# A two-layer decoder trunk on one core: the ten split-weight buffers each at another place within 128 bytes

## The chip, the core and the metric

The kernel runs on one core of a Trainium2 chip. The metric is the device time of one execution in microseconds; the time of a kernel is the median of its runs. Five engines work side by side: TensorE (PE in the profile; PEld are its weight loads), VectorE (DVE), ScalarE (ACT), GpSimd (POOL) and SyncE (SP), which issues the transfers from the chip's main memory. Each takes its own instructions in program order.

## The reference

A decoder of two layers over 256 tokens of width 1024, in float32. Each layer is a token mixer with two kinds of attention in parallel, and a SwiGLU:

```python
proj = x @ w_in      # q, k, v of 8 stick-breaking heads, q, k, v of 8 MoBA heads, two gates
branch_sb = merge_heads(stick_breaking(q_sb, k_sb, v_sb)) @ w_branch_sb
branch_mb = merge_heads(moba(rope(q_mb), rope(k_mb), v_mb)) @ w_branch_moba
mix = (sigmoid(g_sb) * branch_sb + sigmoid(g_mb) * branch_mb) @ w_out
x = layer_norm(ALPHA * x + mix)
x = layer_norm(ALPHA * x + (silu(x @ w_gate) * (x @ w_up)) @ w_down)
```

## The kernel before, in words

The matrix products are done in pieces of 128 rows. To keep float32 accuracy with TensorE's faster 32-bit type, every operand is split into a rounded part (`hi`) and the rest (`lo`), and every product is three matmuls into one bank, written out in `mm3` (L281): hi x hi, hi x lo, lo x hi. All matmuls but the transposes are issued on L275.

The weights of a layer are cut into 122 *granules* of 128 partitions x 1024 float32, 4096 bytes in each partition. `WeightStream.line` takes one granule after another: a transfer into one of four `raw` buffers (L119), the rounded copy `whi` by ScalarE (L145), the rest `wlo` = `raw` - `whi` by VectorE (L149). There are ten buffers for `whi` and ten for `wlo`, and granule g uses buffer g modulo 10 (`NSPLIT`). A granule may be split once the one ten places ahead of it has had its last matmul (`allow`).

A granule is used in one of two ways. A matmul has a *stationary* operand of 128 x 128, which a weight load brings into the array while the matmul before it still runs, and a *moving* operand that streams past it.

- `feat_major` (L327) and the branch projections (L671 on): the weights are stationary, eight slices of 128 columns (512 bytes) per granule, and 256 tokens move. A granule is 24 matmuls of 256 columns. This holds for the q and k of stick-breaking (`pqk`), the gates (`pg`), the branch projections (`pb`) and most of the SwiGLU input (`pf`).
- `tok_major` (L305) and `token_out` (L336): the activations are stationary, and up to 512 columns of the weights move. This holds for `pv`, `pq`, `pk`, `pu`, `pvq`, `pft`, the output projection `pw` and the down projection `pd` and `pe`.

In these names l0 or l1 ahead is the layer. `xT_hi` and `xT_lo` are the transposed tokens.

The order of all instructions is fixed when the program is built, by `Weave`: it walks along the matmuls with an estimate of every engine's clock and puts in the side work (attention, norms, rotary, splits) where its operands should be there. The addresses play no part in this order.

All tiles lie in pools of on-chip memory, at addresses set when the program is built. `xT_hi`, `xT_lo` are in the pool `const`, at a multiple of 128 bytes. The weight buffers follow in `wpool`: four `raw`, ten `whi`, ten `wlo`, each 4096 bytes, all of them at byte 64 of 128. The pools `acts` (attention outputs, gates, SwiGLU outputs, fifteen tiles of 4096 bytes) and `work` come behind it, their large tiles too at byte 64 of 128.

Of the kernel before, what the change touches and what calls it, by code (L numbers as in the profile page):

```python
# [8 lines left out]
F32R = mybir.dt.float32r  # L9
# [5 lines left out]
P = 128  # L15
# [14 lines left out]
GCOLS = 1024  # L30
# [4 lines left out]
class Weave:  # L35
    """Program order: the main line of projections, with side lines (attention, norms,
    rotary, weight splits) woven in. Every engine takes its instructions in program order,
    so each is emitted about when its operands are there, by an estimate of the time at
    which each engine gets through what it has been given. A side line yields the time
    at which it goes on; on the tensor engine's clock."""  # L40

# [40 lines left out]
    def start(self, gen):  # L82
        """A side line whose first stage comes now."""
        side = self.add(gen)
        if not self.busy:
            self._step(side)
        return side
# [9 lines left out]
class WeightStream:  # L97
    """Weight granules [128, 1024]: loaded in float32, then split exactly into
    two float32r parts (hi = rounded, lo = the rest) for the tensor engine."""

# [13 lines left out]
    def load(self, upto):  # L114
        while self.loaded < min(upto, self.total):
# [7 lines left out]
            self.loaded += 1  # L123

    def line(self):
        """The side line: a granule at a time, as far as the buffers allow."""
        nc, weave = self.nc, self.weave
        while self.split < self.total:
            g = self.split
            ahead = g - self.current  # L130
            if g > self.limit:
                yield weave.t + 0.1
                continue
            if ahead >= LEAD and max(weave.dve_t, weave.act_t) > weave.t + BACKLOG:
                yield weave.t + 0.2
                continue
            self.load(g + NRAW)
            if ahead > 0:
                yield self.there[g]
            hi, lo = (self.pool.tile([P, GCOLS], F32R, tag=n, name=f"{n}{g}", bufs=NSPLIT)  # L140
                      for n in ("whi", "wlo"))
            t = self.raw.pop(g)
            n = GCOLS // len(self._pieces(g))
            for sl in self._pieces(g):
                e = weave.act(self.there[g], n, nc.scalar.copy, hi[:, sl], t[:, sl])  # L145
            if g - self.current > 0:
                yield e
            for sl in self._pieces(g):
                e = weave.dve(e, n, nc.vector.tensor_sub, lo[:, sl], t[:, sl], hi[:, sl].bitcast(F32))  # L149
            self.parts[g], self.ready[g] = (hi, lo), e  # L150
            self.split += 1
            self.load(g + 1 + NRAW)

    def allow(self, g):
        """Granule g's buffers are free from here on."""
        self.limit = max(self.limit, min(g, self.total - 1))
# [9 lines left out]
NRAW = 4  # L166
NSPLIT = 10
HOLD = 8
N_WARM = 7
# [10 lines left out]
def hybrid_trunk_kernel(ctx: ExitStack, tc: tile.TileContext, w, xT_in, x_in, ln_in,  # L180
# [6 lines left out]
    work = ctx.enter_context(tc.tile_pool(name="work", bufs=3))  # L187
# [24 lines left out]

# [1 line left out]
    xT_raw = [unit(f"xT_raw{t}", [P, KC, P]) for t in range(2)]  # L214
# [12 lines left out]
    nc.scalar.activation(warm, zero, AF.Sigmoid)  # L227
    # The tensor engine's clock rises after some microseconds of work: give it zeros meanwhile.
    idle = unit("idle", [P, 512], F32R)
# [42 lines left out]

# [1 line left out]
    def mm(o, a, b, start, stop):  # L274
# [30 lines left out]
    def tok_major(o, g, t, first, last, k0):  # L305
        """o[tokens of t, 512] += x @ granule g ([2 kc, 512])."""
        hi, lo = ws.take(g)
        hi = hi.rearrange("p (k c) -> p k c", k=2)
        lo = lo.rearrange("p (k c) -> p k c", k=2)
        for k in range(2):  # L310
            ts = slice(t * P, (t + 1) * P)
            mm3(o, xT_hi[:, k0 + k, ts], xT_lo[:, k0 + k, ts], hi[:, k, :], lo[:, k, :],
                first and k == 0, last and k == 1)

    def both_tokens(name, g0, put):
        """All tokens of x @ granules g0..g0+3; put(tokens, bank) takes each half."""
        acc = [bankM(f"{name}{t}", [P, WIDTH]) for t in range(2)]
        order = ((0, 0), (1, 0), (0, 1), (1, 1), (0, 2), (0, 3)) if g0 == 0 else \
            ((0, 0), (0, 1), (0, 2), (1, 0), (1, 1), (0, 3))
        for t, k in order + ((1, 2), (1, 3)):  # L320
            tok_major(acc[t], g0 + k, t, k == 0, k == 3, 2 * k)
            if t == 1:
                ws.allow(g0 + k + NSPLIT)
            if k == 3:
                put(t, acc[t])

    def feat_major(o, g):  # L327
        """o[128 columns, 256 tokens] = (x @ granule g)^T, g [8 kc, 128 columns]."""
        hi, lo = ws.take(g)
        hi = hi.rearrange("p (k c) -> p k c", k=KC)  # L330
        lo = lo.rearrange("p (k c) -> p k c", k=KC)
        for k in range(KC):
            mm3(o, hi[:, k, :], lo[:, k, :], xT_hi[:, k, :], xT_lo[:, k, :], k == 0, k == KC - 1)
        ws.allow(g + NSPLIT)

    def token_out(o, g, t, s_hi, s_lo, first, last):  # L336
        """o[tokens of t, 1024] += s^T @ granule g ([1 kc, 1024]); o: (first column, bank) ..."""
        hi, lo = ws.take(g)
        ts = slice(t * P, (t + 1) * P)
        for c0, ps in o:  # L340
            cs = slice(c0, c0 + ps.shape[-1])
            mm3(ps, s_hi[:, ts], s_lo[:, ts], hi[:, cs], lo[:, cs], first, last)

    ROWS = [(slice(h * DH, (h + 1) * DH), slice((1 - h) * DH, (2 - h) * DH)) for h in range(2)]

    # Per head, q is stacked as [hi; lo] over the 128 rows and each part of k is there twice,
    # so that q k^T = q_stack (k_hi twice) + q_stack (k_lo twice).
    def stack_q(qs, src, n, c, e):
        """qs[head] [128, ...] from src [2 heads x 64, ...]; the second head is [lo; hi]."""
        for h, (a, b) in enumerate(ROWS):  # L350
            e = act(e, n, nc.scalar.activation, qs[h][a], src[a], AF.Copy, scale=c)
        yield e
        for h, (a, b) in enumerate(ROWS):
            dve(e, n, nc.vector.scalar_tensor_tensor, qs[h][b], src[a], c, qs[h][a].bitcast(F32),
                op0=OP.mult, op1=OP.subtract)
# [15 lines left out]
    def rope_line(name, ps, t, put):  # L371
        """Token-major q or k (8 heads x 64) -> rotary -> transposed, handed to put."""
        tmp = work.tile([P, 8, DH], F32, tag="T", name=f"{name}_tok{t}")
# [22 lines left out]
    def scores(s, q, kh, kl, m):  # L396
        """Scores of both heads of a pair: columns 0:128 = (q0, k0), 128:384 = (q1, k0 k1),
        with the causal mask m added to the diagonal blocks."""
        for h in range(2):
# [12 lines left out]
    def weighted(name, p, wt, v, oT, e):  # L412
        """oT[:, p] = (wt @ v)^T for both heads of pair p."""
        yield e + MARGIN
# [93 lines left out]
    def scale_shift(e, x, cols, sub, op, scale, g, b, e_scale):  # L508
        """x <- ((x op sub) g) scale + b; yields each piece of columns as it is done."""
        for c in cols:  # L510
# [7 lines left out]
    def norm_line(name, t, junk, gb):  # L518
        """x_t <- LN(alpha x_t + ps) g + b, and its transpose into xT (split)."""
        x = xs[t]  # L520
# [26 lines left out]
    def last_norm(name, t, banks, gb, down):  # L547
        """The output's tokens: LN(alpha x_t + sum) g + b, blocks of columns in turn."""
        x = xs[t]
# [24 lines left out]

# [1 line left out]
    norms = []  # L576
    for l in range(DEPTH):
        G = l * NG_LAYER
        L = f"l{l}"

        # v of stick-breaking and q of MoBA: tokens 0..127 first
        v_sb = pair_tiles(L + "vsb", [P, 2, WIDTH])
# [28 lines left out]

        # Each pair of stick-breaking heads starts with its q and k; k and v of MoBA and the
        # first gates come between, MoBA's heads after the last sigmoid of stick-breaking, and
        # the gates' sigmoids after the last exponential of MoBA.
        o_sb = pair_tiles(L + "osb", [P, NPAIR, S])
# [47 lines left out]

        # branch projections and the gated merge, feature-major
        gb = load_gb(l, 0)
# [20 lines left out]

        # output projection: tokens 0..127 first
        norms = []
# [7 lines left out]

        # SwiGLU, first chunks token-major (tokens 0..127 first)
        h_t = [pair_tiles(f"{L}h{i}", [P, 4, S]) for i in range((NFC + 3) // 4)]
# [47 lines left out]

        # down projection: the last granules' tokens 0..127 first
        gb = load_gb(l, 1)
# [5 lines left out]
        g = G + 100  # L754
# [102 lines left out]
```

## Time and profile before

| | |
|---|---|
| median of 3 runs | 753.91 us |
| lowest and highest run | 753.79 and 755.08 us |
| span of the profiled execution, first to last instruction | 747.6 us |
| bytes moved by transfers | 136.31 MB, mean 182 GB/s |
| mean granted TensorE clock | 0.999 |

The profile gives the span of the profiled execution; the time of the runs has 6.3 us more than that span, before its first and behind its last instruction. Busy time of an engine is the time in which at least one of its instructions ran. A matmul's record covers its way through the array, so records overlap, and the distance between the starts of two matmuls is shorter than the length of one. The chain that ended last lists, in order of time, the stretches of work that set the end, each with its start, its length and its count of instructions.

### The profile page before, as it was taken

What the parts mean: (1) busy time and instruction counts of PE and PEld (TensorE: products, weight loads), DVE (VectorE), ACT (ScalarE), POOL (GpSimd) and SP (SyncE); (2) the same over time, 40 slices, a digit from 0 to 9 for tenths busy, and PEclk for the clock granted to TensorE, in tenths of its full rate; (3) what the DMA queues carried; (4) which work ended last, traced back from release to release, by engine and by line L of the source; (5) the groups of instructions that cost most, each with busy time, mean ns of one, the idle gap of its engine ahead of it and who ended that gap; (6) DMA issues with size and microseconds to landing.
All of it is one profiled execution on the core that took longest, in us unless ns stands there. A gap on an engine that the chain in (4) does not pass through costs nothing.

```text
span 747.6 us, 12689 instructions
## 1 busy us (share of the span) xinstructions
PE 735.1 (98%) x5049; PEld 675.5 (90%) x5049; DVE 529.9 (71%) x772; ACT 421.8 (56%) x655; POOL 13.4 (2%) x20
## 2 busy tenths in 40 slices
PE   8999999999999999999999999999999999999996
PEld 5888999998799999988888889999987999999885
DVE  6897878696886666644488878886768866665416
ACT  6788867744565445433267877777435654554300
POOL 0000000000000000000000000000010000000001
PEclk9999999999999999999999999999999999999999
DMA  8864724554586565676168445345635865657501
GB/s 292 284 217 151 221 93 153 176 199 167 178 265 227 181 194 182 198 241 194 60 196 258 146 162 177 108 145 198 210 113 183 277 201 194 196 185 246 166 1 56
DMA packets 39082, 136.31 MB, mean 182 GB/s; under 512 B 4464, under 2 KB 6000, under 8 KB 39024
## 3 DMA queue, kind: packets, MB, share of 16 engines
q1 hardware_dynamic: 39024, 135.51, 55.6%
q8 instruction: 39, 0.64, 0.3%
q14 instruction: 19, 0.16, 0.1%
HBM read 134.45 MB, written 1.05 MB: 181 GB/s over the span
## 4 chain that ended last, share of the span: by engine, by line
PE 84%; DVE 6%; ACT 3%; DMA 3%; issue 2%; POOL 1%; SPq 0%; POOLq 0%; DVEq 0%; ACTq 0%
PE l0pf L275 14%; PE l1pf L275 13%; PE l0pd L275 8%; PE l1pg L275 6%; PE l0pg L275 6%; PE l1pe L275 4%; PE l1pd L275 4%; PE l1pb L275 3%; PE l0pb L275 3%; PE l1pvq L275 3%; DMA raw<-in_w_dram 3%; PE l1pw L275 2%; PE l0pw L275 2%; PE l1pqk L275 2%; DVE wlo L53 2%
## 5 line engine op out<-in xcount | busy, mean ns | idle before, releaser
L53 DVE TENSOR_TENSOR wlo<-raw,whi 128x1024 fp32r<-128x1024 f32 (+1 forms) x245 | 296.8, 1219 | 93.0 <-ACT whi L48 89.5
L48 ACT CAST whi<-raw 128x1024 fp32r<-128x1024 f32 (+1 forms) x245 | 254.1, 1046 | 86.7 <-PE l0pd L275 22.6
L275 PE MATMUL l0pf<-xT_hi,whi 128*128 128x256 f32 x288 | 81.0, 281 | 0.0
L275 PE MATMUL l0pf<-xT_lo,whi 128*128 128x256 f32 x288 | 80.9, 281 | 0.0
L275 PE MATMUL l0pf<-xT_hi,wlo 128*128 128x256 f32 x288 | 80.9, 281 | 0.0
L275 PE MATMUL l1pf<-xT_hi,whi 128*128 128x256 f32 x288 | 79.6, 276 | 0.0
L275 PE MATMUL l1pf<-xT_lo,whi 128*128 128x256 f32 x288 | 79.5, 276 | 0.0
L275 PE MATMUL l1pf<-xT_hi,wlo 128*128 128x256 f32 x288 | 79.5, 276 | 0.0
L275 PEld LDWEIGHTS l0pf<-xT_hi,wlo 128*128 128x128 f32 x288 | 55.3, 192 | 0.0
L275 PEld LDWEIGHTS l0pf<-xT_lo,whi 128*128 128x128 f32 x288 | 54.1, 188 | 0.0
L275 PEld LDWEIGHTS l1pf<-xT_lo,whi 128*128 128x128 f32 x288 | 54.1, 188 | 0.0
L275 PEld LDWEIGHTS l0pf<-xT_hi,whi 128*128 128x128 f32 x288 | 54.1, 188 | 0.0
L275 PEld LDWEIGHTS l1pf<-xT_hi,whi 128*128 128x128 f32 x288 | 54.1, 188 | 0.0
L275 PEld LDWEIGHTS l1pf<-xT_hi,wlo 128*128 128x128 f32 x288 | 54.1, 188 | 0.0
L275 PE MATMUL l0pg<-xT_hi,whi 128*128 128x256 f32 x128 | 35.9, 281 | 0.0
L275 PE MATMUL l1pg<-xT_hi,whi 128*128 128x256 f32 x128 | 35.9, 281 | 0.0
L275 PE MATMUL l0pg<-xT_lo,whi 128*128 128x256 f32 x128 | 35.5, 277 | 0.0
L275 PE MATMUL l1pg<-xT_lo,whi 128*128 128x256 f32 x128 | 35.5, 277 | 0.0
L275 PE MATMUL l1pg<-xT_hi,wlo 128*128 128x256 f32 x128 | 35.4, 277 | 0.0
L275 PE MATMUL l0pg<-xT_hi,wlo 128*128 128x256 f32 x128 | 35.4, 277 | 0.0
L275 PE MATMUL l0pd<-whi,l0h_hi 128*128 128x512 f32 x88 | 34.4, 391 | 0.0
L275 PE MATMUL l0pd<-whi,l0h_lo 128*128 128x512 f32 x88 | 34.3, 389 | 0.0
(379 smaller groups left out, 1821.1 us busy)
## 6 DMA issues: line engine op xcount, KB each, us to landing
raw<-in_w_dram SPq DMA_DIRECT2D x243, 512.0 KB, 4.1
ln<-in_ln_dram SPq DMA_DIRECT2D x8, 512.0 KB, 7.3
xT_raw<-in_xT_dram SPq DMA_DIRECT2D x8, 128.0 KB, 5.0
x<-in_x_dram SPq DMA_DIRECT2D x2, 512.0 KB, 6.4
out_dram<-x SPq DMA_DIRECT2D x3, 256.0 KB, 2.1
raw<-in_w_dram SPq DMA_DIRECT2D x2, 256.0 KB, 3.7
out_dram<-x SPq DMA_DIRECT2D x2, 128.0 KB, 2.0
mask<-in_mask_dram SPq DMA_DIRECT2D x1, 128.0 KB, 3.2
```

What stands on the lines that cost most here:

```text
L48: f(*args, **kw)
L53: f(*args, **kw)
L275: nc.tensor.matmul(o, a, b, start=start, stop=stop)
```

## The change

Each of the twenty buffers gets a tile of its own, 8 float32 longer than a granule, and the granule's data starts at 0 to 6 float32 within it:

```diff
+    def _part(self, n, g):
+
+        i = g % NSPLIT
+        t = self.pool.tile([P, GCOLS + 8], F32R, tag=f"{n}{i}", name=f"{n}{g}", bufs=1)
+        at = PLACES[i]
+        return t[:, at:at + GCOLS]
+
     def line(self):
...
-            hi, lo = (self.pool.tile([P, GCOLS], F32R, tag=n, name=f"{n}{g}", bufs=NSPLIT)
-                      for n in ("whi", "wlo"))
+            hi, lo = (self._part(n, g) for n in ("whi", "wlo"))
...
 NSPLIT = 10
+PLACES = (0, 0, 4, 4, 0, 2, 4, 6, 1, 5)
```

The rest of the diff blanks docstrings and comments and moves the line numbers by seven. On every engine the instructions, their order and their waits are as before; only addresses differ. A tile is now 4128 bytes, and the tiles lie in the order `whi` 0, `wlo` 0, `whi` 1, `wlo` 1 and so on. The built programs have these starts, in bytes modulo 128:

| buffer | 0 | 1 | 2 | 3 | 4 | 5 | 6 | 7 | 8 | 9 |
|---|---|---|---|---|---|---|---|---|---|---|
| `whi`, before | 64 | 64 | 64 | 64 | 64 | 64 | 64 | 64 | 64 | 64 |
| `wlo`, before | 64 | 64 | 64 | 64 | 64 | 64 | 64 | 64 | 64 | 64 |
| `whi`, after | 64 | 0 | 80 | 16 | 64 | 8 | 80 | 24 | 68 | 20 |
| `wlo`, after | 96 | 32 | 112 | 48 | 96 | 40 | 112 | 56 | 100 | 52 |

`xT`, `raw` and all tiles of `const` stay where they were. `acts`, `work` and `small` lie 640 bytes further on, which is a multiple of 128, so their places within 128 bytes are as before.

## The prediction

> **What bounds the kernel.** I read the page first, then the chain that ended last, then the groups of weight loads and of the two splitting engines.
>
> ```profile
> span 747.6 us, 12689 instructions
> PE 735.1 (98%) x5049; PEld 675.5 (90%) x5049; DVE 529.9 (71%) x772; ACT 421.8 (56%) x655; POOL 13.4 (2%) x20
> ...
> PEclk9999999999999999999999999999999999999999
> ...
> PE 84%; DVE 6%; ACT 3%; DMA 3%; issue 2%; POOL 1%; SPq 0%; POOLq 0%; DVEq 0%; ACTq 0%
> ```
>
> TensorE is busy for 98% of the span, its clock is granted in full, and 84% of the chain that ended last is its own time. So the time is, in the main, the number of matmuls times the distance from one start to the next. The busy figures can't give that distance, since matmuls overlap; the chain can, because it lists unbroken runs with their length and count (start, length, what, count):
>
> ```profile
> 77.56 5.44 PE l0pg L275 x48
> ...
> 83.92 5.65 PE l0pqk L275 x48
> ...
> 90.59 3.75 PE l0pg L275 x33
> ...
> 143.10 23.02 PE l0pb L275 x192
> 166.12 17.04 PE l0pw L275 x75
> ...
> 215.20 99.64 PE l0pf L275 x846
> 314.84 55.08 PE l0pd L275 x243
> ...
> 375.61 6.88 PE l1pvq L275 x30
> ...
> 511.20 23.02 PE l1pb L275 x192
> ...
> 583.38 95.90 PE l1pf L275 x846
> ```
>
> Divide length by count. The SwiGLU projection of layer 0 (`l0pf`) takes 99.64 / 846 = 117.8 ns per matmul, that of layer 1 (`l1pf`) 95.90 / 846 = 113.4 ns: the same code, the same shapes, the same 846. The gates `l0pg` go at 113.3 ns, `l0pqk` six microseconds later at 117.7, and the branch projections `l0pb` and `l1pb` at 119.9, each for 23 us on end. All of these have 256 moving columns. So one shape has three speeds, each of which holds for tens of microseconds. With 512 columns `l0pd` takes 226.7 ns, `l0pw` 227.2 and `l1pvq` 229.3. The weight loads show the same split (count, then busy us and mean ns of one):
>
> ```profile
> L275 PEld LDWEIGHTS l0pf<-xT_hi,wlo 128*128 128x128 f32 x288 | 55.3, 192 | 0.0
> L275 PEld LDWEIGHTS l1pf<-xT_hi,wlo 128*128 128x128 f32 x288 | 54.1, 188 | 0.0
> L275 PEld LDWEIGHTS l0pf<-xT_lo,whi 128*128 128x128 f32 x288 | 54.1, 188 | 0.0
> ...
> L275 PEld LDWEIGHTS l0pb<-l0omb_hi,whi 128*128 128x128 f32 x32 | 6.1, 192 | 0.0
> ```
>
> At the fast pitch every load takes 188 ns; in `l0pf` one of three (the low part) takes 192; in `l0pb` all do. I read this as the two streams that TensorE takes from on-chip memory, the load of the next stationary tile and the moving operand of the running matmul, getting into each other's way at some relative positions. In the projections the load comes from a weight buffer at byte 64 of 128 and the moving operand from `xT` at byte 0; in `l0pb` both are at 64. That the chip does this is a reading of these rows, not shown by them: 113.4 and 117.8 occur with the same addresses, so the position alone doesn't decide it.
>
> A rule speaks against this reading. The Trainium skill, "TensorE: Matmul & The Clock Gate", section "Step-by-step: what each phase is for", says that TensorE has two independent read ports and that loading the next tile's weights takes no bandwidth from the running matmul. By it places could not matter and the sum would be zero; the three pitches at a full clock and the loads of 188 and 192 ns are hard to square with it.
>
> **The change part by part.** No instruction is added, removed or moved, on any engine or queue, and the waits are the same: `whi` and `wlo` turned through ten buffers before, and turn through ten now. What changes is where they lie. Before, all twenty start at byte 64 of 128. After, a tile is 32 bytes longer, so each next one starts 32 bytes further on, and `PLACES` adds 0 to 24 bytes. `whi` of slots 0 to 9 starts at byte 64, 0, 80, 16, 64, 8, 80, 24, 68 and 20, `wlo` 32 bytes further. The other large tiles that TensorE reads keep their place of 128.
>
> *The splitting engines.* ScalarE writes `whi`, VectorE reads it and writes `wlo`:
>
> ```profile
> L53 DVE TENSOR_TENSOR wlo<-raw,whi 128x1024 fp32r<-128x1024 f32 (+1 forms) x245 | 296.8, 1219 | 93.0 <-ACT whi L48 89.5
> L48 ACT CAST whi<-raw 128x1024 fp32r<-128x1024 f32 (+1 forms) x245 | 254.1, 1046 | 86.7 <-PE l0pd L275 22.6 <-PE l1pe L275 20.0 <-PE l0pf L275 14.9
> ...
> L53 DVE TENSOR_TENSOR l0sb_beta<-l0sb_beta,l0sb_inc 128x766 f32<-128x766 f32 x4 | 3.8, 957 | 0.4
> ...
> L53 DVE TENSOR_TENSOR l0sb_pl<-l0sb_pT,l0sb_ph 128x768 fp32r<-128x768 f32 x4 | 3.8, 952 | 0.1
> ...
> PE l0pv L275 <- DVE wlo L53: 1.6, 4, 0.8
> ```
>
> `l0sb_beta` reads `inc` from its second float on, four bytes off, and its 766 elements take 957 ns against 952 for 768 of `l0sb_pl`, which starts on the line. So a shifted VectorE read costs at most 5 ns; for 245 that is 1.2 us, in front of which VectorE stood idle for 93.0. A shifted write is shown nowhere; I take zero, the nearest row. At the upper end, ten per cent on ScalarE's 1046 ns is 26 us, within its 86.7 of idle time. The cover is thin only at the start, where TensorE waits for `wlo` four times, 1.6 us in all; there ten per cent on both is below 1 us. I keep 0 to +1.
>
> *Weights as the stationary operand, 256 columns.* By the code these are 864 `pf`, 384 `pg`, 192 `pqk` and 192 `pb` in each layer, 3264 in all. Now granule after granule has another distance between load and moving operand, for `whi` and `wlo` apart, so no speed is handed on for 36 granules as in `pf`. Which place gives which speed no row shows. With a third of the matmuls at each of the three speeds the mean is (113.4 + 117.8 + 119.9) / 3 = 117.0 ns. Against today: `l0pf` 864 x -0.8 = -0.7 us; `l1pf` 864 x 3.6 = +3.1; `pg`, at 113.6 (3.75 / 33), 768 x 3.4 = +2.6; `pqk`, half at each of 113.3 and 117.7, 384 x 1.5 = +0.6; `pb` 384 x -2.9 = -1.1. Sum +4.5. With half at the fast speed and a quarter at each other the mean is 116.1, and the same five terms are -1.5, +2.3, +1.9, +0.2 and -1.5, together +1.4. I take the middle, **+3 us**. The ends: all at the fast speed is -3.8 for `l0pf`, -2.5 for `pb`, -0.8 for `pqk` and -0.2 for `pg`, so -7.3; all at 119.9 is +1.8, +5.6, +4.8 and +1.7, so +13.9.
>
> *Weights as the moving operand, 512 columns.* 576 matmuls have `xT` as stationary operand (`pv`, `pq`, `pk`, `pu`, `pvq`, `pft`), 654 another tile (`pw`, `pd`, the wide `pe`). The first go at about 229.3 ns, the others at about 226.7. If both kinds come to lie between, they cancel: -576 x 1.3 + 654 x 1.3 = +0.1; I take zero. All at 226.7 is -1.5, all at 229.3 is +1.7. The narrow `pe` matmuls, 132, are worth at most 132 x 6.5 = 0.9 and are left at zero.
>
> Sum: +3 us on the profiled span of 747.6. The median of the runs, 753.9, lies 6.3 above the span, and nothing outside the span is touched: 753.9 + 3 = about **757.0**.
>
> **The rivals.**
>
> *The spread breaks the slow lock (faster).* If most distances are harmless, `l0pf` and `pb` come down to 113.4 and the projections to 226.7: -7.3 - 1.5 = -8.8, so 745, and half of it 749.5. For it: in the chain the gates return to 113 ns after nearly every break, so the fast state seems the natural one. Against it: in `l1pf` and the gates there is nothing left to gain.
>
> *A start off the line costs extra (slower).* Seven of ten slots start off a multiple of 32 bytes. If such a start makes each load one step longer, the step is at most what the slowest pitch has over the fastest, 119.9 - 113.4 = 6.5 ns. On 0.7 of the 2880 `pf`, `pg` and `pqk` that is +13.1, less 2.7 that `l0pf` pays today: +10.4, or 764. If the 512-column matmuls pay too, 0.7 x 1230 x 6.5 = +5.6 more: 770. It turns the result slower from a price of about 2 ns on (0.7 x 2880 x 2 = 4.0, which the 2.7 no longer covers). For it: pitch and loads move in steps of several ns, as a memory with wide lines would give. Against it: no row has such a start on TensorE. The Trainium skill, "SBUF — State Buffer", section "Specifications (TRN2)", gives lines of 16 bytes and a penalty for each cross to a new one; by it a 512-byte load off the line touches 33 lines, not 32, in four of the ten slots. No run here shows that price.
>
> *The places do nothing.* The speed is set by how a run is entered, not by places. Then `l0pf` and `l1pf` fall either way again: -3.8 to +3.8 around 753.9.
>
> **How the numbers follow.** The mixture, my forecast, has 0.45, with 754 to 760 as its own range; the broken lock 0.20; the extra step 0.20; nothing 0.15. About 0.2% (1.5 us) is what a measurement of this kernel can tell from no change. Slower by more: 0.27 of the mixture, 0.20 of the extra step, 0.05 of nothing, together 0.52. Same: 0.12 and 0.06, 0.18. Faster: 0.06, 0.20 and 0.04, 0.30. The range runs from 746, almost the whole gain of the broken lock, to 768, between the two prices of the extra step; some 0.1 lies beyond each end at most.
>
> **What would show it.** In the chain of the changed kernel `l0pf` and `l1pf` should come closer to each other, with runs of about 98.5 us for 846, and no longer keep one pitch: within ten granules the pitch should change with the slot. `pb` should be under 23.0 us for 192. ScalarE's 1046 ns and VectorE's 1219 should stand. If all granules of slots 2, 3 and 5 to 9 are slow and 0, 1 and 4 are not, it is the extra step. If `l0pf` or `l1pf` keeps one pitch throughout, places do nothing. The prediction is wrong if the 512-column runs move by more than 2 ns, or if waits on `wlo` appear.

## The result, and the profile after

| | before | after |
|---|---|---|
| median of the runs | 753.88 us (753.79 to 755.08, 4 runs) | 762.15 us (761.74 to 763.08, 4 runs) |
| span of the profiled execution | 747.6 us | 759.3 us |
| time of the profiled execution | not among the runs | 761.76 us |

The change makes the kernel slower by about 1%: the ratio is 1.0106, with an interval of [1.0091, 1.0121]. The forecast was 757.0 with a range of 746 to 768.

The page of the changed kernel: its span, busy times, granted clock, and the shares of the chain that ended last.

```profile
span 759.3 us, 12689 instructions
...
PE 748.2 (99%) x5049; PEld 684.9 (90%) x5049; DVE 530.9 (70%) x772; ACT 421.6 (56%) x655; POOL 13.4 (2%) x20
...
PEclk9999999999999999999999999999999999999998
...
PE 87%; DVE 4%; ACT 4%; issue 2%; DMA 1%; SPq 1%; POOL 1%; POOLq 0%; DVEq 0%; ACTq 0%
...
L53 DVE TENSOR_TENSOR wlo<-raw,whi 128x1024 fp32r<-128x1024 f32 (+1 forms) x245 | 296.8, 1219 | 95.5 <-ACT whi L48 92.1
L48 ACT CAST whi<-raw 128x1024 fp32r<-128x1024 f32 (+1 forms) x245 | 253.8, 1045 | 88.4 <-PE l0pd L282 23.6
...
L282 PEld LDWEIGHTS l0pf<-xT_hi,wlo 128*128 128x128 f32 x288 | 54.3, 188 | 0.0
```

TensorE's busy time grew by 13.1 us and the span by 11.7, at nearly the same granted clock (0.999 before, 0.996 after). ScalarE and VectorE take what they took (1045 and 1219 ns for a granule). TensorE's waits for `wlo`, by the view of waits (total us, times, longest):

```profile
PE l0pv L282 <- DVE wlo L53: 1.3, 2, 0.8
```

They were 1.6 us in four. So nobody waits longer; the matmuls lie further apart. The chain of the changed kernel (start, length, what, count) shows which:

```profile
78.03 5.66 PE l0pg L282 x48
...
84.60 5.69 PE l0pqk L282 x48
...
145.14 22.64 PE l0pb L282 x192
167.78 17.49 PE l0pw L282 x75
...
217.54 100.21 PE l0pf L282 x846
317.75 56.46 PE l0pd L282 x243
...
380.00 7.01 PE l1pvq L282 x30
...
590.10 100.14 PE l1pf L282 x846
```

With 256 columns these runs now have nearly one mean pitch (distance from one start to the next): `l0pf` 118.5 ns, `l1pf` 118.4, the first gates 117.9, `l0pb` 117.9. With 512 columns `l0pd` rose from 226.7 to 232.3, `l0pw` from 227.2 to 233.2, `l1pvq` from 229.3 to 233.7.

The mean hides a pattern that the starts of the single matmuls show. From the second granule on `l0pf` repeats the same pitches every ten granules: 117.5 to 118.8 ns in nine slots and 121.1 in slot 9. No granule of 256 columns in the changed kernel has a mean pitch below 116.7 ns.

The span grew by 11.7 us and the time by 8.3, because the profiled execution of the kernel before wasn't typical of its runs. The first experiment shows that.

### The profile page after: what moved, and what is told of

It is laid out like the page before. It is cut to its first block, busy times and chain, and to the rows that moved or that the text cites. A ratio compares the mean times of both kernels' runs of the same rounds, so it can differ in the third digit from the quotient of the medians.

```text
span 759.3 us, 12689 instructions
## 1 busy us (share of the span) xinstructions
PE 748.2 (99%) x5049; PEld 684.9 (90%) x5049; DVE 530.9 (70%) x772; ACT 421.6 (56%) x655; POOL 13.4 (2%) x20
## 4 chain that ended last, share of the span: by engine, by line
PE 87%; DVE 4%; ACT 4%; issue 2%; DMA 1%; SPq 1%; POOL 1%; POOLq 0%; DVEq 0%; ACTq 0%
PE l0pf L282 13%; PE l1pf L282 13%; PE l0pd L282 8%; PE l0pg L282 6%; PE l1pg L282 6%; PE l1pe L282 4%; PE l1pd L282 4%; PE l1pb L282 3%; PE l0pb L282 3%; PE l1pvq L282 3%; PE l0pw L282 2%; PE l1pw L282 2%; PE l0pqk L282 2%; PE l1pqk L282 2%; PE l1pft L282 2%; PE l0pft L282 2%
## 5 line engine op out<-in xcount | busy, mean ns | idle before, releaser
L53 DVE TENSOR_TENSOR wlo<-raw,whi 128x1024 fp32r<-128x1024 f32 (+1 forms) x245 | 296.8, 1219 | 95.5 <-ACT whi L48 92.1
L48 ACT CAST whi<-raw 128x1024 fp32r<-128x1024 f32 (+1 forms) x245 | 253.8, 1045 | 88.4 <-PE l0pd L282 23.6
```

The costliest lines, as they stand in the source:

```text
L48: f(*args, **kw)
L53: f(*args, **kw)
```

## The experiments

All but the first change addresses or add a few transposes; the matrix products are those of the kernel before. Places are start addresses. Up to `acts0` they were thought of modulo 128, as in the prediction. Each run's expectation is quoted first.

**`before_again`: the kernel before, unchanged.**

> The kernel before, unchanged, profiled a second time. Between its runs (753.9 us) and its span (747.6) lie 6.3 us, but after the change only 2.5 (761.8 and 759.3). Theory: the profiled execution shown of it was a lucky one, in which l1pf ran at 113.4 ns per matmul; in the usual run l1pf goes at 117.8 like l0pf, which adds 864 x 4.4 = 3.8 us. Then this span is 751.4 and the time 753.9. Rival: what lies outside the span varies; then the span is 747.6 again and l1pf takes 95.9 us for 846.

Measured: 753.86 us (750.19 to 755.03, 10 runs), ratio 1.001 [0.9984, 1.0037]. The 23 runs of the kernel before that were made on one chip, these ten and 13 beside them, gather in two places: 11 are below 751.5 and 11 at 753.7 or more, with one between. The chain of the profiled execution, which took 754.03 us with a span of 751.7:

```profile
215.81 99.64 PE l0pf L275 x846
...
583.80 99.64 PE l1pf L275 x846
```

In the first profile of the same kernel `l1pf` took 95.90 us. The same code at the same addresses has it at 113.4 ns in one execution and at 117.8 in another, 3.7 us apart, and every other group of matmuls agrees within 0.2 us once waits are set apart. So the first profile showed the shorter kind of execution and the median is of the longer. What lies outside the span is 754.03 - 751.7 = 2.3 us, not 6.3. A median, and a ratio to it, depends on how many of the runs beside it were of which kind, so below the times and the pitches say more than the ratios.

With this profile as the base the loss can be laid out. The distances between the starts of consecutive matmuls in both traces are summed by group; a distance over 140 ns with 256 columns, or over 262 with 512, counts as 118 or 232 and the rest of it as a wait. From `before_again` to the changed kernel: 512 columns +5.2 us, gates +3.0, `pf` +1.2, `pqk` +1.0, `pb` -0.7, narrow `pe` -0.1, waits and all other matmuls -2.0. Sum +7.6, as the spans say (759.3 - 751.7). Another bound for a wait moves a few tenths between the terms.

**`w0`: all weights at byte 0 of 128.** Two pads of 64 bytes around the weight buffers of the kernel before, so that the activations move by 128:

```diff
+            if g == 0:
+                self.pool.tile([P, 16], F32, tag="pad0", name="pad0", bufs=1)
             hi, lo = (self.pool.tile([P, GCOLS], F32R, tag=n, name=f"{n}{g}", bufs=NSPLIT)
                       for n in ("whi", "wlo"))
+            if g == 0:
+                self.pool.tile([P, 16], F32, tag="pad1", name="pad1", bufs=1)
```

> All twenty weight buffers at byte 0 of 128 instead of 64, everything else in its place. Theory 'distance' (the reading of the prediction: a load and a moving operand at distance 0 go at 119.9 ns, at distance 64 at 113.4 or 117.8): pf, pg and pqk, now at distance 0 from xT, go at 119.9, and pb, now at distance 64, at 113.4 to 117.8; about +14 and -2 us, 766. Theory 'change' (what costs is that the place changes from one operand to the next; with one place for all a run settles into a steady pitch): every run keeps one steady pitch, and the time is within 4 us of 753.9. Theory 'off the line': no start is off a multiple of 32 bytes, 753.9.

Measured: 762.5 us (762.2 to 762.79), ratio 1.013 [1.0094, 1.0166]. From its chain:

```profile
145.67 22.61 PE l0pb L279 x192
...
218.08 100.39 PE l0pf L279 x846
318.47 56.69 PE l0pd L279 x243
...
591.21 100.40 PE l1pf L279 x846
```

The whole loss is there with one uniform place, at a multiple of 128 bytes, so neither changing places from granule to granule nor a start off the line is needed for it. `pf` is at 118.7 ns, `pd` at 233.3. No theory had it: 'distance' gave the loss, but by 119.9 ns in `pf` and nothing at 512 columns.

**`p0`: the change with all of `PLACES` zero.** The tiles still step by 32 bytes. The edit is against the kernel before, with a `_part` as in the change:

```diff
+        t = self.pool.tile([P, GCOLS + 8], F32R, tag=f"{n}{i}", name=f"{n}{g}", bufs=1)
+        at = PLACES[n][i]
...
+PLACES = {"whi": (0, 0, 0, 0, 0, 0, 0, 0, 0, 0), "wlo": (0, 0, 0, 0, 0, 0, 0, 0, 0, 0)}
```

> The change with PLACES all zero: tiles of 4128 bytes, so whi lies at 64 or 0 and wlo at 96 or 32, by turns; no start off a multiple of 32 bytes. Theory 'off the line': nothing is left of the loss, 753.9. Theory 'change': hi and lo still differ and so do neighbouring granules, so the matmuls of 256 columns stay at about 118.3 ns as after the change and the time is about 760 to 762. Theory 'distance': granules at distance 0 (odd ones, whi) slow, the others mixed, about 757.

Measured: 759.69 us (759.52 to 760.76), ratio 1.0096 [1.006, 1.0132], span 758.6, `l0pf` 99.89 us for 846. Most of the loss stands without a single start off a multiple of 32, so the extra step of the second rival isn't its main part.

**`s32`: both parts of a granule at one place, stepping by 32 bytes** (`PLACES` zero as in `p0`, and the pad `pad1` of `w0` behind the first granule's two tiles, so the first step is 96 bytes).

```diff
+        t = self.pool.tile([P, GCOLS + (8 if n == "wlo" else 0)], F32R, tag=f"{n}{i}", name=f"{n}{g}", bufs=1)
...
+            hi, lo = (self._part(n, g) for n in ("whi", "wlo"))
+            if g == 0:
+                self.pool.tile([P, 16], F32, tag="pad1", name="pad1", bufs=1)
```

> whi and wlo of one granule at the same place, the next granule 32 bytes further on (64, 32, 64, 96, 0, 32, 64, 96, 0, 32). Theory 'change': within a granule of 24 matmuls nothing changes, so the pitch settles inside each granule and only the first few matmuls of it pay; about 755 to 757, clearly less than p0. Theory 'distance': pitch goes by the slot and is the same in each turn of ten granules; the granules at byte 0 go at 119.9; about 757, as p0. Theory 'off the line': 753.9.

Measured: 761.08 us (760.74 to 761.4), ratio 1.0111 [1.0076, 1.0147], `l0pf` 100.24 us for 846. All three theories gave too short a time. By the starts each slot has its own pitch, the same turn after turn in `l0pf` (117.3 to 120.2 ns), as 'distance' said. Single granules of slots 0, 2 and 6 reach 113.3, but no set of slots stayed fast.

**`x64w0`: `xT` moved from byte 0 to 64 of 128, the weights from 64 to 0.** A pad of 64 bytes ahead of `xT` in `const`, which moves the weights too, and one behind the weights:

```diff
+            if g == 0:
+                self.pool.tile([P, 16], F32, tag="pad1", name="pad1", bufs=1)
             t = self.raw.pop(g)
...
+    const.tile([P, 16], F32, name="xpad")
     xT_hi = const.tile([P, KC, S], F32R, name="xT_hi")
```

> The kernel before with xT moved from byte 0 to byte 64 of 128 and all weight buffers from 64 to 0: the distance between load and moving operand is the same as before, each place is not. Theory 'distance' (the pitch of 256 columns hangs on the distance of the two operands): l0pf, l1pf and the gates keep the pitches of before, 113.3 or 117.8 ns, and pb, now at distance 64, leaves 119.9 for 117.8 or 113.3; the 512-column matmuls, whose moving operand now lies at 0, go to 233 ns as with all weights at 0 (576 x 3.8 + 654 x 6.4 = +6.4 us), so about 757 to 760 us. Theory 'own place' (each operand's place counts by itself): load at 0 is slow, pf and gates at 118 to 119 ns as with all weights at 0 and xT at 0, so 762 or more.

Measured: 749.45 us (748.87 to 750.56), ratio 0.9933 [0.9918, 0.9948]. From its chain:

```profile
143.72 22.61 PE l0pb L278 x192
...
215.85 95.91 PE l0pf L278 x846
311.76 56.69 PE l0pd L278 x243
...
390.01 7.58 PE l1pvq L278 x33
...
582.00 95.90 PE l1pf L278 x846
```

With the weights at byte 0, as in `w0`, `pf` now has the fast pitch of 113.4 ns in both layers. Of the operands of the matrix products only `xT` lies elsewhere than in `w0`, by 64 bytes. So the place of the weights doesn't count by itself; their distance from `xT` does. The expectation missed at 512 columns: `pd` did go to 233.3 ns, but `l1pvq`, with its moving operand at byte 0 too, kept 229.7.

**`x64`: `xT` moved, so that weights, `xT` and activations all start at 64 of 128.** The pad ahead of `xT` moves all that follows by 64 bytes, and a second one brings the weights back to 64 of 128. They and the activations thus lie 128 bytes further on than before.

```diff
+            if g == 0:
+                self.pool.tile([P, 16], F32, tag="pad0", name="pad0", bufs=1)
             hi, lo = (self.pool.tile([P, GCOLS], F32R, tag=n, name=f"{n}{g}", bufs=NSPLIT)
                       for n in ("whi", "wlo"))
...
+    const.tile([P, 16], F32, name="xpad")
     xT_hi = const.tile([P, KC, S], F32R, name="xT_hi")
```

> The kernel before with xT alone moved from byte 0 to byte 64 of 128, so that weights, xT and all activations start at 64. Theory 'distance': pf, gates and q/k, now at distance 0, go at the 119.9 ns that pb has in the kernel before: l0pf +1.8 us, l1pf +1.8 to +5.6, gates +4.8, q/k +0.9, together +9 to +13; the 576 matmuls of 512 columns with xT as stationary operand go from 229 to 226.7, -1.5; so 760 to 765 us. Theory 'own place' (weights at 64 are fast to load whatever the moving operand's place): nothing changes at 256 columns, about 752 us.

Measured: 760.66 us (759.95 to 762.48), ratio 1.0086 [1.0068, 1.0105]. From its chain:

```profile
145.47 23.03 PE l0pb L278 x192
...
217.79 100.39 PE l0pf L278 x846
318.19 55.12 PE l0pd L278 x243
...
394.98 7.69 PE l1pvq L278 x33
```

With the weights at 64 of 128 as before, `pf` loses its fast pitch. But it goes at 118.7 ns, not at the 119.9 of `pb`, which also has distance 0 of 128; and `l1pvq` at 233.0, not at 226.7.

**`acts0`: the activations moved from 64 to 0.** A pad behind the weight buffers:

```diff
+            if g == 0:
+                self.pool.tile([P, 16], F32, tag="pad1", name="pad1", bufs=1)
             t = self.raw.pop(g)
```

> The kernel before with all activations (the branch outputs, the merged tokens, h) moved from byte 64 to byte 0 of 128; weights stay at 64, xT at 0. Theory 'distance': pb, now at distance 64, goes from 119.9 to 117.8 or 113.3 ns, 23.0 to 22.6 or 21.8 us for 192; the 512-column matmuls with an activation as stationary operand (pw, pd, wide pe) go from 226.7 to the 229 that those with xT at 0 have, 654 x 2 = +1.3 us; the rest stands: within 1.5 us of the kernel before. Theory 'own place': pb keeps 119.9, as its load stays at 64.

Measured: 754.06 us (749.37 to 754.71, 10 runs), ratio 0.9985 [0.9969, 1.0]. From its chain:

```profile
145.60 22.61 PE l0pb L277 x192
...
317.38 56.70 PE l0pd L277 x243
...
587.51 95.90 PE l1pf L277 x846
```

`pb` came down to 117.8 ns as expected. `pd` went to 233.3, where 229 was expected. That the time is none the less that of the kernel before is chance: against `before_again` the 512-column matmuls cost 3.9 us more, and `l1pf` fell into the fast pitch, 3.7 us less.

These three misses have one answer: the modulus is 256. The addresses of the built programs give, in the kernel before, the weights and activations at 192 of 256 and `xT` at 128; in `x64` they are 64 and 192. Sort every uniform layout by the next load's start minus the running matmul's moving start, modulo 256, and each distance has its own pitch in long runs:

| distance | 256 columns | 512 columns |
|---|---|---|
| 0 | 119.9 (`pb` before) | 226.7 (`pd` before) |
| 64 | 113.4 or 117.8 (`pf` before, `x64w0`) | 233.3 (`pd` in `w0`, `x64w0`, `acts0`) |
| 128 | 118.7 (`pf` in `w0`, `x64`) | 232.5 to 233.0 (`pq`, `l1pvq` in `x64`) |
| 192 | 117.8 (`pb` in `w0`, `x64w0`, `acts0`) | 229.3 (`l1pvq` before) |

**`w128`: the weights moved by 128 bytes, nothing else.** Every tile keeps its place of 128; only the modulus of 256 sees a difference. The pads of `w0` with twice the size (the activations behind them move by 256):

```diff
+                self.pool.tile([P, 32], F32, tag="pad0", name="pad0", bufs=1)
...
+                self.pool.tile([P, 32], F32, tag="pad1", name="pad1", bufs=1)
```

> The kernel before with all weight buffers moved by 128 bytes and nothing else: every tile keeps its place of 128. Theory 'distance of 128' (what counts is load minus moving operand modulo 128): nothing changes, about 750 or 754 us as the kernel before. Theory 'distance of 256' (modulo 256, as the six layouts run so far group it): pf, gates and q/k come from distance 64 to 192 and go at the 117.8 ns that pb had there, so l1pf +3.7 where it was fast, gates +2.6, q/k +0.5; pb comes from 0 to 128 and goes at 118.7, -0.5; the 512-column matmuls with xT as stationary operand come from 192 to 64, 229.2 to 233.3 ns, 576 x 4.1 = +2.4; pw, pd and the wide pe from 0 to 128, 226.9 to 232.5, 654 x 5.6 = +3.7. Sum +8.7 on the slower of the kernel before's two times: about 762 us.

Measured: 760.59 us (760.1 to 763.26), ratio 1.0087 [1.0056, 1.0118]. From the chain of the profiled execution, which was the longest of the four and had 1.7 us more of waits than `before_again`, those of `pv` and `pq` at the start:

```profile
148.08 22.79 PE l0pb L279 x192
...
220.59 99.64 PE l0pf L279 x846
320.23 56.46 PE l0pd L279 x243
...
382.47 7.01 PE l1pvq L279 x30
...
592.22 99.64 PE l1pf L279 x846
```

`pf` 117.8 ns, `pb` 118.7, `pd` 232.3, `l1pvq` 233.7: four pitches called from the table (117.8, 118.7, 232.5, 233.3) and met within 0.4 ns. `pf` alone wouldn't tell, since 117.8 is also the slow pitch of distance 64; the other three do. A distance modulo 128 falls.

One entry of the table is not the whole of it. At distance 192 most stretches go at 117.8 ns, but a few short ones don't:

```profile
34.78 2.73 PE l0pqk L279 x24
```

That is 113.8 ns. So distance 192, like 64, has a fast pitch too, though no long run was seen in it.

**`own0`: the change with tiles of 4096 bytes and no offsets**, so that each buffer has its own tag but the place of 256 that it had before. The edit is `p0`'s but for the length of a tile:

```diff
+        t = self.pool.tile([P, GCOLS + 0], F32R, tag=f"{n}{i}", name=f"{n}{g}", bufs=1)
```

> The change without its places: ten buffers with a tag of their own, but 4096 bytes each and no offset, so that all start at the same place of 256 as in the kernel before. Theory 'distance': the places alone make the loss, so 750 or 754 us, l1pf at 113.4 or 117.8 ns, l0pd at 227. Theory 'own buffers' (the ten tags change what waits for what): about 760, the loss of the change.

Measured: 754.25 us (750.25 to 756.3, 10 runs), ratio 1.0 [0.9981, 1.0019]. The profiled execution was one of the shorter ones:

```profile
315.01 55.08 PE l0pd L281 x243
...
583.18 95.90 PE l1pf L281 x846
```

The ten tags cost nothing. All of the loss is in the places.

**`e8`: the change without the two slots that start 4 bytes off a multiple of 8.**

```diff
-PLACES = (0, 0, 4, 4, 0, 2, 4, 6, 1, 5)
+PLACES = (0, 0, 4, 4, 0, 2, 4, 6, 0, 4)
```

> The change with the last two of PLACES, (1, 5), set to (0, 4): slots 8 and 9 no longer start 4 bytes off a multiple of 8. Theory 'four bytes off costs the moving operand' (in the trace of the change 512-column matmuls with such a start take 236 to 239 ns beside 232 to 234): a fifth of 1230 x 4.5 ns = -1.1 us, so about 761 us, and slots 8 and 9 at 232 to 234 ns. Theory 'chance of the lock': no difference, 762.

Measured: 760.61 us (760.31 to 762.02), ratio 1.0095 [1.0061, 1.0128]; span 758.4 against 759.3 of the change. From the chain of `e8`, where the changed kernel has 56.46 us in the first row and 7.01 and 7.75 for the last two:

```profile
317.48 56.34 PE l0pd L282 x243
...
379.56 7.01 PE l1pvq L282 x30
...
395.56 7.68 PE l1pvq L282 x33
```

By the sums over the starts the 512-column matmuls cost 0.9 us less than in the change (+4.3 on `before_again` against +5.2) and `pf` 0.6 less. That is 0.9 / 246 = 3.7 ns for a 512-column matmul whose moving operand started 4 bytes off, close to the 4.5 expected. In `l0pf` slot 9 falls from 121.1 to 117.4 ns.

**`kick6`: the kernel before with four more transposes ahead of the two that break each `pf` run** (the same product, written again).

```diff
             pe_after(e)
+            for i in (0, 1, 0, 1) if j == 1 and t == 1 else ():
+                nc.tensor.transpose(tp[:, i, :], sg[:, i * P:(i + 1) * P], ident)
             for i in range(2):
                 transpose(tp[:, i, :], sg[:, i * P:(i + 1) * P])
```

> The kernel before with four more 128-column transposes ahead of the two that break each layer's pf run (the same product written thrice; the result is the same). Theory 'entry': two pitches are possible at the same places, the pitch is set where a run is entered, and the gates go back to 113.3 ns after six transposes while pf goes slow after two; so l0pf goes from 117.8 to 113.3 ns behind the six (-3.6 us), l1pf is fast too (0 or -3.7), and the eight more transposes cost 0.5 us: 747 to 750 us. Theory 'chance' (what the run falls into has nothing to do with the break): l0pf 117.8 as in all runs of the kernel before, time +0.5.

Measured: 747.33 us (747.16 to 748.25), ratio 0.9906 [0.9891, 0.9921]. From its chain:

```profile
143.70 23.02 PE l0pb L275 x192
...
216.23 95.90 PE l0pf L275 x846
...
580.88 95.90 PE l1pf L275 x846
```

Eight transposes of 0.9 us in all bring 7.5 us in `pf` against `before_again`. No address moved, so which of the two pitches of distance 64 a run takes is set by what comes just ahead of it; whether the number of transposes counts or the time they take wasn't separated. This version beats both kernels, and its four runs, within 1.1 us, show one time instead of two.

**`after_kick6`: the same transposes in the changed kernel.**

> The change with the four more transposes ahead of the two that break each layer's pf run, as in kick6. Theory 'distance': with a new distance at each granule there is no fast pitch to be entered; l0pf and l1pf stay at 118 ns and the time is that of the change plus 0.5 for the transposes, about 762.5 us. Theory 'entry alone' (the change lost its time by entering the runs badly): l0pf and l1pf fall to 113.4 ns, -8 us, about 754.5.

Measured: 762.86 us (762.67 to 763.84), ratio 1.0122 [1.0095, 1.0148]. From its chain:

```profile
218.45 100.21 PE l0pf L282 x846
...
591.46 100.13 PE l1pf L282 x846
```

Nothing is won: +0.9 us for the transposes and `pf` as without them. In the changed kernel this entry leads to no fast pitch.

## Why the prediction fell short in size, and had its sign by luck

- **The bound** was right: TensorE's pitch sets the time, before and after. **The splitting engines** were right at about zero: 1045 and 1219 ns stand, and the four waits on `wlo` became two.
- **The reading of the two streams**, that the relative place of load and moving operand sets the pitch, was right in kind (`x64w0` and `x64` show it). Two things in it were wrong. The places were taken modulo 128; `w128` shows 256. By that modulus the activations didn't keep their place in the change either: 640 bytes are 128 more, so they moved from 192 to 64. And the loads of 188 and 192 ns are no sign of the pitch: the changed kernel loads in 188 at 118.5 ns.
- **The rule of the Trainium skill** that the prediction set against its reading ("TensorE: Matmul & The Clock Gate", section "Step-by-step: what each phase is for": two independent read ports, so that a load takes nothing from the running matmul) doesn't hold here as the prediction applied it, that places could not matter. From `w0` to `x64w0` `xT` is the only operand of the products that moves, by 64 bytes and with no added work, and `pf` goes from 118.7 to 113.4 ns.
- **256 columns, the first step that failed.** The prediction gave each of three seen speeds a third, or half to the fast one, so a mean of 116.1 to 117.0 ns and +3 us. Those speeds came from two of the distances, 0 and 64. In long runs the other two go at 118.7 and 117.8, and the fast speed was held only at distance 64 with the right entry. The share given to the fast speed was the mistake: no granule of 256 columns in the changed kernel has it. The measured mean in `pf` is 118.4. Against the profile that the sum started from, these four groups cost +8.5 us in place of +3 (3.7 of it in `l1pf`, which that profile had in its shorter kind).
- **512 columns, the second.** Taken as zero, within -1.5 and +1.7, by the thought that the two kinds, 226.7 and 229.3, would meet in between. They don't bound what can happen: they are the two best of four distances, 0 and 192, and the other two take 232.3 to 233.7. Measured: +5.3 us against that profile, of which the starts 4 bytes off are 0.9. The text had named a move of more than 2 ns as the sign of its failing; it was 4 to 6.
- **The offset, the third.** The forecast added 6.3 us between span and runs; it was 2.5 after the change (761.76 - 759.3), the rest being mostly the `l1pf` of one execution. This made the forecast too high by 3.8 and hid over a third of the shortfall: +8.5 - 3 = +5.5 and +5.3 from the matmuls, less 3.8 and less 2.1 of waits and other matmuls, are 4.9 of the 5.2 us by which 762.15 stands over 757.0; the rest is the 0.4 by which that median is above the profiled execution, less rounding.
- **The sign was luck.** Without those 3.8 us the same sum gives about 753, not above the 753.88 of the kernel before. Seen from an execution like `before_again`, in which `l1pf` goes at 117.8 ns already, the forecast's own mean speeds make `l1pf` faster by 0.7 or 1.5 us where the sum had it slower by 3.1 or 2.3. The slower result came from pitches that the forecast didn't have.
- **The signs it had named.** The pitch does change with the slot, as told. `l0pf` and `l1pf` came together, but at 100.2 us for 846 where 98.5 was told.
- **`pqk` and `pb`** came roughly as told: `pqk` slower by 1.1 (told +0.2 to +0.6), `pb` faster by 0.7 (told -1.1 to -1.5).
- **The rivals.** The broken lock fails: the spread keeps every run off the fast pitch. That places do nothing fails with `own0` beside the change. The extra step doesn't show in the slots that the prediction named for it: slots 0 and 4, which it left out, take 118.6 and 118.8 ns in `l0pf`, and slots 2 and 3, which it named, 117.7 and 117.8. A price for starts off the line exists, but it is small and clear only at 4 bytes: grouped by the moving operand's start modulo 16, the 512-column matmuls of the changed kernel take about 232 ns at 0, 233 at 8 and 236 at 4; with 256 columns, by the load's start, 118.1, 118.2 and 119.1. The distances differ between these sets too, so `e8` is the measurement. The Trainium skill's "SBUF — State Buffer", section "Specifications (TRN2)", with a penalty for each crossed line of 16 bytes, would charge a start at 8 as well as one at 4; the runs show a clear price for the second alone, 3.7 ns by `e8`.

What stays open: why these distances have these pitches (that the two streams meet in on-chip memory is argued, not shown), whether a long run at distance 192 can be brought into the fast pitch, what makes `l1pf` of the kernel before fall into one pitch or the other from execution to execution, and the exact pitch of distances between the multiples of 64, where only mixtures were run. That `pb` at distance 64 would reach 113.4 ns wasn't tried, as its operands come from one pool with those of `pd`, which is fastest at distance 0.

## What to carry to other kernels

When the chain shows the same matmul at several steady pitches under a full clock, note for each the address distance of load and moving operand, modulo 256 at least, before forecasting a new layout; speeds seen at two distances don't bound a third. Check on several runs whether the profiled execution is a typical one, by the lengths of its longest unbroken runs, before its span is set against the median. And where one layout has two pitches, a cheap break ahead of a long run can choose the better one: 0.9 us of transposes brought 7.5 here, where both long runs had the slow one.

## What the runs showed of the hardware that was not expected

- At a granted clock of 0.994 or more in every profile quoted, 256-column matmuls of this type had steady pitches from 113.4 to 119.9 ns and 512-column ones from 226.7 to 233.7 where all starts were multiples of 64 bytes, by the distance of two addresses modulo 256. The order of the distances isn't the same for both: 64 is best for 256 columns and worst for 512.
- One program at fixed addresses took either about 750 or about 754 us from execution to execution, by the pitch into which a single run of 846 matmuls fell. In each of its profiles the pitch held through the whole run.
